# The opening of a two-layer transformer trunk: who sums the modulation weights, and in which number format the first projection runs

## The chip, the cores and the metric

The program runs on one core of a Trainium2 chip. The metric is the device time of one execution in microseconds (us). The kernel before was timed in three runs: median 2475.24 us, lowest 2470.18, highest 2477.14.

## What is computed

Two layers work on 256 tokens of 2048 features in float32. Every sub-layer normalises its input, multiplies it by a scale and adds a shift, and the scales and shifts come from a conditioning vector `c` through a large matrix `ada_w`. The opening of the program is the first of these steps and the projection behind it:

```
mod = einsum('bd,lde->lbe', silu(c), ada_w) + ada_b        # (2 layers) x 2048 x 12288
shift_m, scale_m, gate_m, shift_f, scale_f, gate_f = split(mod[layer], 6)
h = rmsnorm(x, norm_g[layer, 0]) * (1 + scale_m) + shift_m
proj = h @ a_w_in                                          # 2048 -> 512 + 256 + 128 + 16
q_lat, c_kv, k_idx, w_idx = split(proj)                    # each but the last is normalised
q_idx = q_lat @ a_w_idx_qb                                 # the indexer's queries, 16 heads
...                                                        # selection of keys, attention, MLP, layer 1
```

For layer 0 the opening needs the columns of `ada_w` that give `shift_m` and `scale_m`: 2048 rows by 4096 columns, 32 transfers of 1024 KB. `a_w_in` adds 16 pieces of 456 KB and `x` 8 pieces of 256 KB.

## The kernel before, in words

Everything is unrolled in one function, `trunk`. A library orders the instructions of each engine, gives each tile its memory and places the waits. Each engine then runs its own list in order, and the transfers are issued from the list of SyncE (SP).

**The opening** goes through the features in eight segments of two chunks (`SEG = 2`, a chunk is 128 features). One `step` loads 8 chunks of rows (`ROWS`) of 256 columns of `ada_w` for one part (scale or shift) of a segment: one transfer of 1024 KB (`start_load`, L501), five steps ahead of its use (`LEAD`), into one of six buffers. There are 32 steps, four per segment. `start_sum` then weighs the rows with silu(c) and adds them up. VectorE (DVE) takes four of the eight rows of a step (`ROWS_DVE`), one instruction per row of 128x256 (`add_row`, L206 for the first, L208 after it). TensorE (PE) takes the other four as matmuls that give one row of 256 sums (`row`, L511).

When a segment's sums are done, `start_columns` copies the row out of PSUM (ScalarE, L525) and `ada_columns` brings both kinds of sums into columns by tiny matmuls (`col`, L227 and L228), after which VectorE adds the bias and forms gain times (1 + scale) (`mod`, L229 and L232). `start_project` modulates the transposed x (`xT`) of the two chunks. `start_product` multiplies them with `a_w_in`.

The product comes in two forms. For the first twelve chunks (`LATE = 12`) the weights and the features are each split into a high and a low part in the format float32r (`halves` and `split`: L131 on ScalarE, L132 on VectorE), and three matmuls stand for one (L553 to L555). For the last four chunks the matmul is in plain float32 (L546). The results collect in PSUM: `pq` (512 columns) and `pk` (400 columns) for two token tiles each.

**Behind the opening** the tiles of the opening's pool are given back (`sp_.close()`), and layer 0's attention begins. For each of the two token tiles the loop from L625 on takes the norm of `pq`, transposes it and splits it into `qlat`. In the same pass it does the same for the keys' part in `pk` (`ckv`, `kidx`). The power in `inv_rms` runs on GpSimd (POOL, L139), which also issues the transfers of the position bias (L736). Then the indexer loops over four units of `a_w_idx_qb`: `unit` fetches two raw tiles (`fetch`, L106; four raw buffers in all), splits them (L131, L132), and lets the `Filler` tick. The filler spreads the sums for all later modulations over the program: its loads `adaw` are 512 KB each (L272), its sums are VectorE instructions of 128x1024 (L208). The products of the unit with `qlat` are `qi` (L126 to L128), and `dots` (L678) needs `kidx`.

Of the kernel before, what the change touches and what calls it, by code (L numbers as in the profile page):

```python
# [39 lines left out]
SEG = 2  # L40
ROWS = 8
ROWS_DVE = 4
LATE = 12
# [3 lines left out]
def trunk(ctx: ExitStack, tc: tile.TileContext, x, c, rel_bias, ada_w, ada_b, norm_g, a_w_in, a_q_norm,  # L47
# [14 lines left out]
    # ---------------------------------------------------------------- constants  # L62
# [30 lines left out]
    # ---------------------------------------------------------------- weights  # L93
# [48 lines left out]
    # ---------------------------------------------------------------- per-feature columns  # L142
# [16 lines left out]
    banks(f=(0, 1), m=(2, 3), lg=(4, 5), s=(6,), av=(7,), row=(4, 5, 7))  # L159
# [32 lines left out]
    # relative position bias by distance, then by (query, key)  # L192
# [7 lines left out]
    # ---------------------------------------------------------------- adaLN  # L200
# [9 lines left out]
    def ada_columns(l, p, c0, acc, row=None):  # L210
        """Columns c0 .. of part p (shift, or gain * (1 + scale)) from sums by partition and a row to add."""
# [5 lines left out]
        if row is None:  # L217
            for j in range(0, n, 4):
                ps = small_ps("col")
                for k in range(4):  # L220
                    nc.tensor.transpose(ps[:, k * P:(k + 1) * P], acc[:, (j + k) * P:(j + k + 1) * P], ident)
                nc.vector.reduce_sum(col[:, j:j + 4], ps.rearrange("p (a b) -> p a b", a=4), axis=AX.X)
            sums = col
        else:
            sums = small_ps("col")[:, :n]
            for k in range(n):
                nc.tensor.matmul(sums[:, k:k + 1], acc[:, k * P:(k + 1) * P], ones[:, 0:1], start=True, stop=False)  # L227
                nc.tensor.matmul(sums[:, k:k + 1], row[0:1, k * P:(k + 1) * P], ones[0:1, 0:1], start=False, stop=True)  # L228
        nc.vector.tensor_add(col, sums, bcols[l][:, p * NC + k0:p * NC + k0 + n])  # L229
# [4 lines left out]
    def ada_gate(l, p, c0, acc):  # L234
        """Columns c0 .. of a gate times the norm's gain, in every partition."""
# [20 lines left out]
    class Filler:  # L256
        """Spreads the sums over ada_w's rows between the units of weights; its loads run ahead."""
# [64 lines left out]
    def m_piece(u, xk, ps_tiles, n, tiles=range(NT)):  # L322
        """ps_tiles[t] (tokens, features) += x @ W over u: a list of (k, high, low)."""
# [71 lines left out]
    def x_transposed(r, j, half, tag, xn):  # L395
        """Features (4 * j + 2 * half) * 128 .. of the normalised x, transposed: [P, 2, tokens] in PSUM."""
# [18 lines left out]
    def next_h(a, b):  # L415
        """Tiles for the modulated, normalised x, transposed; and what fills them when a token tile of x is done."""
# [37 lines left out]
    def quiet(what="hold"):  # L454
        """What comes in here waits until the next features are on their way."""
# [17 lines left out]
    def first_products(ps_tiles, ws):  # L473
        """ps_tiles[t] = x @ W over the first chunks, in plain float32, which needs no parts."""
# [7 lines left out]
    # ---------------------------------------------------------------- start: layer 0's first modulation and projection  # L482
    hts = [sp.tile([P, 4, 2, T], F32R, tag=f"h{j}", name=uid("h")) for j in range(LATE // 4)]
# [4 lines left out]
    acc, prow, wa = {}, {}, {}  # L488
    raws = {}
# [3 lines left out]
    SW = SEG * P  # L493
    steps = [(g, p, k) for g in range(NC // SEG) for k in range(0, NC, ROWS) for p in (1, 0)]
    last_step = {g: i for i, (g, _, _) in enumerate(steps)}

    def start_load(i):
        g, p, k = steps[i]
        c0 = p * D + g * SW
        wa[i] = sp.tile([P, ROWS, SW], F32, tag="w", name=uid("w"), bufs=LEAD + 1)  # L500
        nc.sync.dma_start(out=wa[i], in_=rows(ada_w[0], k, k + ROWS, c0, c0 + SW))  # L501

    def start_sum(i):
        g, p, k = steps[i]
        if k == 0:
            acc[g, p] = sp.tile([P, BLK], F32, tag="acc", name=uid("acc"), bufs=4)
            prow[g, p] = small_ps("row", "row")
        for j in range(ROWS_DVE):
            add_row(acc[g, p][:, :SW], wa[i][:, j], k + j, cs)
        for j in range(ROWS_DVE, ROWS):  # L510
            nc.tensor.matmul(prow[g, p][0:1, :SW], cs[:, k + j:k + j + 1], wa[i][:, j],  # L511
                             start=(k == 0 and j == ROWS_DVE), stop=(k + j == NC - 1))

# [8 lines left out]
    def start_columns(g):  # L522
        for p in (1, 0):
            row = sp.tile([1, BLK], F32, tag="row", name=uid("row"), bufs=2)
            nc.scalar.activation(row[:, :SW], prow[g, p][0:1, :SW], AF.Copy)  # L525
            ada_columns(0, p, g * SW, acc[g, p][:, :SW], row)

    def start_project(g):
        a, b = mods[0, 1], mods[0, 0]
        for k in range(g * SEG, (g + 1) * SEG):  # L530
            if k >= LATE:
                modulate(k, h_late[:, k - LATE], xT[:, k], a[:, k:k + 1], b[:, k:k + 1])
                waiting.append((k,))
                continue
            hi, lo = win.pop(k)
            hv = hts[k // 4][:, k % 4]
            h32 = work.tile([P, T], F32, tag="h32", name=uid("h32"))
            modulate(0, h32, xT[:, k], a[:, k:k + 1], b[:, k:k + 1])
# [531 lines left out]
```

## Time and profile before

| What | Value |
|---|---|
| median of three runs | 2475.24 us (2470.18 to 2477.14) |
| span of the profiled execution | 2471.3 us |
| PE / PE weight loads | 98% / 84% of the span |
| DVE / ACT / POOL | 69% / 49% / 2% |
| transfers | 614.21 MB, 249 GB/s over the span |

The span runs from the first to the last instruction of one profiled execution. The page gives no time of its own for that execution beside the span; the median of the timed runs is 3.9 us above it. Busy shares are averages over the span, and PE's ends are modelled. In the rows below, PEld is the loading of weights into TensorE, SPq is a transfer's issue on SyncE, and PEclk is the granted clock of TensorE as a share of its full speed.

### The profile page before, as it was taken

How to read it: one execution, taken by the hardware profiler on the slowest of the kernel's cores; microseconds unless marked ns; L12 is line 12 of the kernel's file. 1: busy time of each engine (PE TensorE's matmuls, PEld its weight loads, DVE VectorE, ACT ScalarE, POOL GpSimd, SP SyncE). 2: the span in 40 equal slices, each digit the busy share in tenths (PEclk: the TensorE clock that was granted, in tenths of full speed). 3: DMA queues.
4: the chain of work that ended last, by engine and by line, in shares of the span. 5: the costliest groups of instructions: out<-in, count | busy, mean ns of one | idle time of the engine just before them, and what ended most of it. 6: DMA issues, size and time to landing. Idle time of an engine off the chain costs nothing.

```text
span 2471.3 us, 37142 instructions
## 1 busy us (share of the span) xinstructions
PE 2409.8 (98%) x14540; PEld 2077.5 (84%) x14540; DVE 1699.2 (69%) x2147; ACT 1203.0 (49%) x1717; POOL 48.5 (2%) x86
## 2 busy tenths in 40 slices
PE   7989999999999999999999999999999999999998
PEld 4559788877988989989977989887898998988986
DVE  5669888888566766766568668877854456655455
ACT  4135755556444444444446554446654444444443
POOL 0010000000000000000000000000000000000000
PEclk9999999999999999999999999999999999999999
DMA  9967988875778878878566788886676557766564
GB/s 354 311 229 244 328 272 308 299 248 196 260 232 280 286 252 294 282 260 283 186 206 208 256 279 322 325 314 221 220 247 191 183 189 240 241 189 187 183 189 145
DMA packets 294472, 614.21 MB, mean 249 GB/s; under 512 B 19492, under 2 KB 60792, under 8 KB 294296
## 3 DMA queue, kind: packets, MB, share of 16 engines
q1 hardware_dynamic: 290464, 603.14, 72.5%
q0 software_dynamic: 3168, 8.53, 1.2%
q8 instruction: 114, 1.87, 0.3%
q14 instruction: 62, 0.51, 0.1%
q10 hardware_dynamic: 664, 0.17, 0.0%
HBM read 609.62 MB, written 2.15 MB: 248 GB/s over the span
## 4 chain that ended last, share of the span: by engine, by line
PE 60%; DVE 3%; DMA 3%; ACT 2%; issue 1%; POOL 0%; SPq 0%; DVEq 0%; POOLq 0%; ACTq 0%
PE m L331 9%; PE m L330 9%; PE m L329 9%; PE f L128 7%; PE f L126 7%; PE f L127 7%; PE pq L128 1%; PE pq L126 1%; PE pq L127 1%; DMA adaw<-in_ada_w_dram 1%; PE pk L128 1%; PE pk L127 1%; PE pk L126 1%; DVE wlo L132 1%; DMA raw<-in_b_w_out_dram 1%
## 5 line engine op out<-in xcount | busy, mean ns | idle before, releaser
L132 DVE TENSOR_TENSOR wlo<-raw,whi 128x1024 fp32r<-128x1024 f32 (+1 forms) x738 | 886.3, 1219 | 447.3 <-ACT whi L131 442.4
L131 ACT ACTIVATE whi<-raw 128x1024 fp32r<-128x1024 f32 (+1 forms) x738 | 767.4, 1055 | 852.4 <-PE f L127 328.3
L128 PE MATMUL f<-h,wlo 128*128 128x256 f32 x1920 | 541.6, 282 | 0.0
L126 PE MATMUL f<-h,whi 128*128 128x256 f32 x1920 | 541.4, 282 | 0.0
L127 PE MATMUL f<-h,whi 128*128 128x256 f32 x1920 | 540.8, 282 | 0.0
L208 DVE SCALAR_TENSOR_TENSOR acc<-adaw,cs,acc 128x1024 f32<-128x1024 f32 x300 | 384.2, 1281 | 74.4 <-DMA adaw<-in_ada_w_dram 71.6
L331 PE MATMUL m<-wlo,hid 128*128 128x512 f32 x1016 | 401.2, 395 | 0.5 <-DVE wlo L132 0.5
L329 PE MATMUL m<-whi,hid 128*128 128x512 f32 x1016 | 401.2, 395 | 0.0
L330 PE MATMUL m<-whi,hid 128*128 128x512 f32 x1016 | 400.8, 395 | 0.0
L127 PEld LDWEIGHTS f<-h,whi 128*128 128x128 f32 x1920 | 361.8, 188 | 1.5
L126 PEld LDWEIGHTS f<-h,whi 128*128 128x128 f32 x1920 | 361.9, 188 | 1.2
L128 PEld LDWEIGHTS f<-h,wlo 128*128 128x128 f32 x1920 | 361.5, 188 | 0.0
L331 PEld LDWEIGHTS m<-wlo,hid 128*128 128x128 f32 x1016 | 191.2, 188 | 46.7 <-DVE wlo L132 1.7
L330 PEld LDWEIGHTS m<-whi,hid 128*128 128x128 f32 x1016 | 191.2, 188 | 43.9
L329 PEld LDWEIGHTS m<-whi,hid 128*128 128x128 f32 x1016 | 191.2, 188 | 43.6
L363 DVE TENSOR_TENSOR y<-m,y 128x512 f32<-128x512 f32 x200 | 136.6, 685 | 31.9 <-PE m L331 31.7
L329 PE MATMUL m<-whi,o 128*128 128x512 f32 x368 | 150.2, 408 | 0.0
L331 PE MATMUL m<-wlo,o 128*128 128x512 f32 x368 | 146.9, 401 | 0.2 <-DVE wlo L132 0.2
L330 PE MATMUL m<-whi,o 128*128 128x512 f32 x368 | 147.0, 399 | 0.0
L331 PEld LDWEIGHTS m<-wlo,o 128*128 128x128 f32 x368 | 69.3, 189 | 15.1 <-DVE wlo L132 0.6
L329 PEld LDWEIGHTS m<-whi,o 128*128 128x128 f32 x368 | 69.6, 189 | 13.5 <-ACT qkv L723 0.3
L330 PEld LDWEIGHTS m<-whi,o 128*128 128x128 f32 x368 | 69.5, 189 | 13.3
(289 smaller groups left out, 3043.6 us busy)
## 6 DMA issues: line engine op xcount, KB each, us to landing
raw<-in_mlp_w_dram SPq DMA_DIRECT2D x504, 512.0 KB, 4.7
adaw<-in_ada_w_dram SPq DMA_DIRECT2D x320, 512.0 KB, 6.4
raw<-in_b_w_in_dram SPq DMA_DIRECT2D x92, 512.0 KB, 5.4
w<-in_ada_w_dram SPq DMA_DIRECT2D x32, 1024.0 KB, 7.1
raw<-in_a_w_out_dram SPq DMA_DIRECT2D x64, 512.0 KB, 5.8
raw<-in_b_w_out_dram SPq DMA_DIRECT2D x32, 512.0 KB, 7.2
raw<-in_a_w_qb_dram SPq DMA_DIRECT2D x16, 512.0 KB, 5.4
raw<-in_a_w_in_dram SPq DMA_DIRECT2D x12, 456.0 KB, 7.3
```

The costliest lines, as they stand in the source:

```text
L126: nc.tensor.matmul(o, sh, mh, start=start, stop=False, skip_group_check=True)
L127: nc.tensor.matmul(o, sh, ml, start=False, stop=False, skip_group_check=True)
L128: nc.tensor.matmul(o, sl, mh, start=False, stop=stop, skip_group_check=True)
L131: return (nc.scalar.activation(dst_hi, src, AF.Copy).ins, nc.vector.tensor_sub(dst_lo, src, dst_hi.bitcast(F32)).ins)
L132: nc.vector.tensor_sub(dst_lo, src, dst_hi.bitcast(F32)).ins)
L208: nc.vector.scalar_tensor_tensor(acc, w, cs[:, k:k + 1], acc, op0=ALU.mult, op1=ALU.add)
L329: nc.tensor.matmul(o, xh[:, ts_], hi, start=(k == 0), stop=False)
L330: nc.tensor.matmul(o, xl[:, ts_], hi, start=False, stop=False)
L331: nc.tensor.matmul(o, xh[:, ts_], lo, start=False, stop=(k == n - 1))
L363: nc.vector.tensor_add(y, pt[d][t], y)
```

## The change

The opening is rewritten. VectorE sums all rows, except the last chunk of rows, which goes to TensorE. A segment now holds four chunks of features (three segments) or two (the last two), and scale and shift stand side by side, so that one instruction adds 1024 columns, or 512 in the last two segments. A step still fills one buffer of 1024 KB, now by two transfers of 512 KB; the last two steps are half as large. `a_w_in` comes in one transfer per segment into two buffers, and all its products are in plain float32, one chunk after each step (two in the short segments). The first two units of `a_w_idx_qb` are fetched and split at the end of the opening, and the norms of `pq` go ahead of those of `pk`. The remaining lines of the diff only take out comments.

```diff
-SEG = 2
-ROWS = 8
-ROWS_DVE = 4
-LATE = 12
+SEGS = ((0, 4), (4, 4), (8, 4), (12, 2), (14, 2))
...
+    for g, (_, n) in enumerate(SEGS):
+        r = 8 // n
+        rs = [r] * (NC // r) if g < len(SEGS) - 1 else [r] * (NC // r - 1) + [r // 2] * 2
+        steps += [(g, sum(rs[:i]), r_) for i, r_ in enumerate(rs)]
...
     def start_load(i):
+        g, k, r = steps[i]
+        k0, n = SEGS[g]
+        w = sp.tile([P, 4 * BLK], F32, tag="w", name=uid("w"), bufs=LEAD + 1)
+        wa[i] = w[:, :2 * r * n * P].rearrange("p (r a n) -> p r a n", r=r, a=2)
+        for p in range(2):
+            c0 = p * D + k0 * P
+            nc.sync.dma_start(out=wa[i][:, :, p], in_=rows(ada_w[0], k, k + r, c0, c0 + n * P))
+
+    def start_w_in(g):
+        k0, n = SEGS[g]
+        w = sp.tile([P, 4, WIN], F32, tag="win", name=uid("win"), bufs=2)
+        nc.sync.dma_start(out=w[:, :n], in_=rows(a_w_in[0], k0, k0 + n, 0, WIN))
...
     def start_sum(i):
+        on_pe = 1 if i == len(steps) - 1 else 0
...
+        for j in range(r - on_pe):
+            add_row(a_, wa[i][:, j].rearrange("p a n -> p (a n)"), k + j, cs)
+        for j in range(r - on_pe, r):
+            for c_ in range(2 * n):
+                nc.tensor.matmul(ps[:, c_:c_ + 1], wa[i][:, j, c_ // n, (c_ % n) * P:(c_ % n + 1) * P],
+                                 cs[:, k + j:k + j + 1], ...)
+        if last:
+            for c_ in range(2 * n):
+                nc.tensor.matmul(ps[:, c_:c_ + 1], a_[:, c_ * P:(c_ + 1) * P], ones[:, 0:1], ...)
...
+    def start_h(g):
+        nc.vector.tensor_add(mod[:, :, ks], acc[g][1][:, :2 * n].rearrange(...), b_)
+        nc.vector.scalar_tensor_tensor(mod[:, 1, ks], mod[:, 1, ks], 1.0, gcol[:, ks], op0=ALU.add, op1=ALU.mult)
+        h = sp.tile([P, 4, T], F32, tag="h", name=uid("h"), bufs=2)
+        for i in range(n):
+            modulate(i if n == 2 else 1, h[:, i], xT[:, k], mod[:, 1, k:k + 1], mod[:, 0, k:k + 1])
+
+    def start_product(k, o, w_, c0, t):
+        nc.tensor.matmul(o[t][:, :w_], h32s[k][:, t * P:(t + 1) * P], win[k][:, c0:c0 + w_],
+                         start=(k == 0), stop=(k == NC - 1))
...
     for i in range(len(steps) + LEAD):
         if i < len(steps):
             start_load(i)
+            g, k, _ = steps[i]
+            if k == 4:
+                start_w_in(g)
...
         start_sum(done)
+        g = steps[done][0]
+        if done - 1 == last_step.get(g - 1):
+            start_h(g - 1)
+            waiting += range(SEGS[g - 1][0], sum(SEGS[g - 1]))
+        for _ in range(1 if SEGS[g][1] == 4 else 2):
+            if waiting:
+                k = waiting.pop(0)
+                for t in range(NT):
+                    for o in outs:
+                        start_product(k, *o, t)
...
+    start_h(len(SEGS) - 1)
+    waiting += range(SEGS[-1][0], NC)
+    for o in outs:
+        for t in range(NT):
+            for k in waiting:
+                start_product(k, *o, t)
+    qi_units = [halves(fetch(rows(a_w_idx_qb[0], 0, 4, u * BLK, (u + 1) * BLK), 4, BLK), 4, BLK) for u in range(2)]
     sp_.close()
```

## Rows read from the trace of the kernel before

**Rows 1.** The page, part 1: busy time, share of the span and instructions of each engine.
```profile
PE 2409.8 (98%) x14540; PEld 2077.5 (84%) x14540; DVE 1699.2 (69%) x2147; ACT 1203.0 (49%) x1717; POOL 48.5 (2%) x86
```
**Rows 2.** Stretches: length, busy us of PE, PEld, DVE, ACT, POOL, PEclk, DMA share, GB/s.
```profile
2.00:40.00 38.00, 27.00 (x107) 13.89 (x108) 18.75 (x52) 19.98 (x42) 3.43 (x9) 0.87 1.06 376
40.00:120.00 80.00, 75.36 (x356) 43.98 (x354) 51.15 (x118) 15.67 (x30) 0.55 (x1) 1.00 0.95 326
140.00:150.00 10.00, 9.13 (x37) 3.98 (x35) 2.30 (x7) 1.88 (x4) 0.00 (x0) 1.00 0.00 0
154.00:156.00 2.00, 2.00 (x4) 1.01 (x3) 1.47 (x2) 0.02 (x1) 0.00 (x0) 0.52 0.73 205
```
**Rows 3.** Transfers in 160 to 170 us, slices of 0.25 us and issues.
```profile
DMA packets 1144, 3.81 MB, mean 381 GB/s; under 512 B 145, under 2 KB 145, under 8 KB 1144
...
adaw<-in_ada_w_dram SPq DMA_DIRECT2D x2, 512.0 KB, 5.4
```
**Rows 4.** SyncE's waits in 0 to 260 us: total, times, longest.
```profile
SPq L501 <- DVE acc L208: 44.8, 18, 4.5
...
SPq L501 <- PE row L511: 28.5, 12, 4.0
```
**Rows 5.** DVE's waits in 40 to 120 us: total, times, longest.
```profile
DVE mod L229 <- PE col L228: 26.4, 10, 4.8
```
**Rows 6.** Groups by shape in 0 to 160 us: busy, mean ns, idle before.
```profile
L511 PE MATMUL row<-w,cs 128*1 128x256 f32 x256 | 64.2, 396 | 1.4 <-DMA w<-in_ada_w_dram 1.4
L208 DVE SCALAR_TENSOR_TENSOR acc<-w,cs,acc 128x256 f32<-128x256 f32 x112 | 53.1, 483 | 2.8
...
L132 DVE TENSOR_TENSOR wlo<-raw,whi 128x1024 fp32r<-128x1024 f32 x4 | 4.8, 1221 | 0.0
```
**Rows 7.** Groups by shape, DVE, 30 to 180 us: the filler's sums.
```profile
L208 DVE SCALAR_TENSOR_TENSOR acc<-adaw,cs,acc 128x1024 f32<-128x1024 f32 x6 | 7.7, 1278 | 0.0
```
**Rows 8.** Timeline of SyncE: start, us, the issues of the opening's end.
```profile
90.99 13.45 SPq L501 DMA_DIRECT2D w<-in_ada_w_dram  x4
...
123.30 0.38 SPq L501 DMA_DIRECT2D w<-in_ada_w_dram  x1
123.78 32.09 SPq L106 DMA_DIRECT2D raw<-in_a_w_idx_qb_dram  x8
```
**Rows 9.** Timeline of 118 to 185 us: the end of the opening.
```profile
123.20 0.50 PE L553 MATMUL pq<-whi,h 128*128 128x512 f32 x1
...
125.88 1.89 PE L511 MATMUL row<-w,cs 128*1 128x256 f32 x8
127.69 0.30 PEld L227 LDWEIGHTS col<-ones,acc 128*128 128x128 f32 x2 [0.44 <-issue]
...
140.85 1.12 PE L546 MATMUL pq<-win,h_late 128*128 128x512 f32 x2
...
144.11 1.89 PE L511 MATMUL row<-w,cs 128*1 128x256 f32 x8
...
151.53 0.60 ACT L410 ACTIVATE h_late<-xT,mod,mod 128x256 f32<-128x256 f32 x1 [0.78 <-DVE mod L229]
...
152.00 1.61 PE L546 MATMUL pq<-win,h_late 128*128 128x512 f32 x2 [0.70 <-DVE h_late L411]
...
157.91 0.60 ACT L625 ACTIVATE sq<-pq 128x512 f32<-128x512 f32 x1 [3.89 <-PE pq L546]
```
**Rows 10.** Timeline of 160 to 200 us: the norms and the first products behind them.
```profile
160.09 1.50 POOL L736 DMA_DIRECT2D bias<-tab_d  x2
...
163.06 0.69 DVE L132 TENSOR_TENSOR qlat<-h,qlat 128x512 fp32r<-128x512 f32 x1
...
168.47 0.68 DVE L132 TENSOR_TENSOR qlat<-h,qlat 128x512 fp32r<-128x512 f32 x1
...
169.21 0.58 PE L127 MATMUL qi<-qlat,whi 128*128 128x256 f32 x1 [0.91 <-DVE qlat L132]
...
176.56 1.47 PE L678 MATMUL dots<-misc,qkv 128*128 128x128 f32 x8
```

More of the change, by code (lines that the diff above doesn't have):

```diff
@@ L216, in ada_columns @@
         col = mods[l, p][:, k0:k0 + n]
[L217 to L229, printed above, removed]
+        for j in range(0, n, 4):
+            ps = small_ps("col")
+            for k in range(4):
+                nc.tensor.transpose(ps[:, k * P:(k + 1) * P], acc[:, (j + k) * P:(j + k + 1) * P], ident)
+            nc.vector.reduce_sum(col[:, j:j + 4], ps.rearrange("p (a b) -> p a b", a=4), axis=AX.X)
+        nc.vector.tensor_add(col, col, bcols[l][:, p * NC + k0:p * NC + k0 + n])
         if p in (1, 4):
@@ L487, in trunk @@
     pk = [bank("f", "pk") for _ in range(NT)]
[L488 to L495, printed above, removed]
-    def start_load(i):
[L498 to L501, printed above, removed]
+    mod = const.tile([P, 2, NC], F32, name="mod_start")
@@ L503, in start_sum @@
+    def start_w_in(g):
+        k0, n = SEGS[g]
+        w = sp.tile([P, 4, WIN], F32, tag="win", name=uid("win"), bufs=2)
+        nc.sync.dma_start(out=w[:, :n], in_=rows(a_w_in[0], k0, k0 + n, 0, WIN))
+        win.update((k0 + i, w[:, i]) for i in range(n))
     def start_sum(i):
-        g, p, k = steps[i]
+        g, k, r = steps[i]
+        n = SEGS[g][1]
+        on_pe = 1 if i == len(steps) - 1 else 0
         if k == 0:
-            acc[g, p] = sp.tile([P, BLK], F32, tag="acc", name=uid("acc"), bufs=4)
-            prow[g, p] = small_ps("row", "row")
@@ L508, in start_sum @@
[L508 to L512, printed above, removed]
+            acc[g] = (sp.tile([P, 2 * BLK], F32, tag="acc", name=uid("acc"), bufs=2)[:, :2 * n * P],
+                      bank("col", "col"))
+        a_, ps = acc[g]
+        for j in range(r - on_pe):
+            add_row(a_, wa[i][:, j].rearrange("p a n -> p (a n)"), k + j, cs)
@@ new lines, in start_sum @@
+        last = i == last_step[g]
+        for j in range(r - on_pe, r):
+            for c_ in range(2 * n):
+                nc.tensor.matmul(ps[:, c_:c_ + 1], wa[i][:, j, c_ // n, (c_ % n) * P:(c_ % n + 1) * P],
+                                 cs[:, k + j:k + j + 1], start=(c_ == 0), stop=False,
+                                 skip_group_check=True)
+        if last:
+            for c_ in range(2 * n):
+                nc.tensor.matmul(ps[:, c_:c_ + 1], a_[:, c_ * P:(c_ + 1) * P], ones[:, 0:1],
+                                 start=(on_pe == 0 and c_ == 0), stop=True, skip_group_check=True)
@@ L520, in start_x @@
                 nc.scalar.activation(xT[:, 4 * j + 2 * half:4 * j + 2 * half + 2], ps, AF.Copy)
[L522 to L538, printed above, removed]
-            split(hv[:, 0], hv[:, 1], h32)
-            waiting.append((k, hi, lo))
@@ L599, in trunk @@
             nc.gpsimd.dma_start(out=tab_d, in_=tab)
-        if done == 1:
-            *bcols, gcol, qncol = [columns(*r_) for r_ in small_rows]
-    while waiting:
-        start_product(*waiting.pop(0))
+    start_h(len(SEGS) - 1)
[5 more added lines that the diff above has]
+    qi_units = [halves(fetch(rows(a_w_idx_qb[0], 0, 4, u * BLK, (u + 1) * BLK), 4, BLK), 4, BLK) for u in range(2)]
     sp_.close()
@@ L620, in trunk @@
     widx = const.tile([P, NT, HI], F32, name="widx")
+    sums = [small.tile([P, NB], F32, tag="ss", name=uid("ss")) for _ in range(NT)]
     for t in range(NT):
         tsl = slice(t * P, (t + 1) * P)
-        ss = small.tile([P, NB], F32, tag="ss", name=uid("ss"))
+        ss = sums[t]
         sq = work.tile([P, BLK], F32, tag="sq", name=uid("sq"), bufs=1)
         nc.scalar.activation(sq, pq[t], AF.Square, accum_out=ss[:, 0:1])
-        nc.scalar.activation(sq[:, :KVR], pk[t][:, :KVR], AF.Square, accum_out=ss[:, 1:2])
         r = inv_rms(ss[:, 0:1], QR)
@@ L635, in trunk @@
         split(qlat[:, :, 0, tsl], qlat[:, :, 1, tsl], h32)
+    for t in range(NT):
+        tsl = slice(t * P, (t + 1) * P)
+        ss = sums[t]
+        sq = work.tile([P, BLK], F32, tag="sq", name=uid("sq"), bufs=1)
+        nc.scalar.activation(sq[:, :KVR], pk[t][:, :KVR], AF.Square, accum_out=ss[:, 1:2])
         r = inv_rms(ss[:, 1:2], KVR)
@@ L667, in trunk @@
     for u in range(4):
-        parts = unit(rows(a_w_idx_qb[0], 0, 4, u * BLK, (u + 1) * BLK), 4, BLK, 1.5)
+        if u < len(qi_units):
+            parts = qi_units[u]
+            filler.tick(1.5)
+        else:
+            parts = unit(rows(a_w_idx_qb[0], 0, 4, u * BLK, (u + 1) * BLK), 4, BLK, 1.5)
         pf = [bank("f", "qi") for _ in range(2)]
```

63 lines of the change are left out of this document (19 added, 44 removed).

## The prediction

> **What bounds the kernel now.** I read the busy shares first: TensorE is busy for 98% of the span [rows 1], so a stretch saved ahead of it is kept unless another engine takes over. Then the stretches of the opening. From 2 to 40 us the transfers run at 376 GB/s, from 40 to 120 us at only 326, and from 140 to 150 us at nothing, though the opening's products are not done [rows 2]. So the opening is not bound by its bytes alone. The waits of SyncE say what holds them: its issues of ada_w's pieces wait 44.8 us for VectorE's sums and 28.5 us for TensorE's row matmuls, the two readers that must let go of a buffer [rows 4]. TensorE is the late one of them: 75 of 80 us busy from 40 to 120 [rows 2], VectorE 51, and VectorE itself stands 26.4 us waiting for column matmuls [rows 5] that lie behind TensorE's other work. A segment takes (123.30 - 90.99) / 2 = 16.2 us [rows 8].
>
> At the end this becomes a tail. The last piece of ada_w is issued at 123.30 [rows 8], but TensorE still works off row matmuls and products (125.88, 140.85, 144.11), the last features are modulated at 151.53, and ScalarE reads the first finished `pq` at 157.91 [rows 9]. The indexer's products run without a break from 169.21 on [rows 10]. The raw buffers are full meanwhile, hence the 10 us without transfers.
>
> **What the change does to the engines.** TensorE loses the row matmuls, 64.2 us [rows 6], and the columns of their rows. A chunk's products cost 125.88 - 123.20 = 2.68 us in three float32r matmuls and 144.11 - 140.85 = 3.26 in plain float32 [rows 9], so twelve chunks cost 12 x 0.58 = 7 us more. All sixteen make 52 us, far under the opening's length.
>
> VectorE loses 53.1 us of sums [rows 6] with the splitting of w_in, and gains 48 sums of 1024 columns at 1.28 us [rows 7] and 32 of 512. The latter has no row; between 0.48 us for 256 [rows 6] and 1.28 for 1024, a straight line gives 0.75. Together 61 + 24 = 85 us, which fits under the transfers if these take 115. In a long segment it is 20.5 us of sums against 27 of transfers, in a short one 12 against 13.6.
>
> **The stream.** 33.6 MB of ada_w, 7.5 of a_w_in and 2.1 of x are 43.1 MB. With TensorE no longer holding buffers I take the 376 GB/s of 2 to 40 us, when buffers were free [rows 2]. That is 115 us, an end at 117. The lower bound is 326 GB/s: an end at 134. SyncE issues 66 transfers for ada_w instead of 32, and 5 for a_w_in instead of 16; at 0.38 us for an issue [rows 8] that is some 27 us of its 117, covered. The pieces become 512 KB: the filler's pieces of that size, beside others, ran at 381 GB/s [rows 3]. (The Trainium skill, "DMA: Bandwidth & Descriptors", section "Bandwidth", says to batch transfers to 1 MiB or more and gives 341 GB/s for that size; by that figure the end would be at an estimated 128 us. Rows 3 speak against it.)
>
> **The last segments, step by step.** At 376 GB/s the long segments land at 35 (x is in the first), 62 and 89.5 us, the short ones at 103 and 117. Third segment: two sums, 2.6 us, to 92.1. Eight column matmuls at 0.30 [rows 9], 2.4, to 94.5. The modulation about 1 us: 0.47 from its start to the product [rows 9] and 0.5 allowed for the two small VectorE steps ahead of it. So its four chunks start at 95.5 and take 13 us, plus 2 because TensorE begins at half clock after a slack stretch (0.52 in 154 to 156 us [rows 2]; the products from 152.00 ran slow for 4 us [rows 9]). TensorE is through at 110.5.
>
> Here the change adds a wait. a_w_in has two buffers, and the fifth segment's piece needs the third segment's. On SyncE's queue stand behind it the last three pieces of ada_w, 2.1 MB. With the 0.9 MB of a_w_in they take 8 us plus some 2 to the landing, from 110.5 to 121 instead of 117. The fourth segment's columns also wait for those products; its two chunks then run from about 112.5 to 119.
>
> From 121: one sum on VectorE 0.75, four columns 1.2, modulation 1, two matmuls of `pq` 1.7 (about half a chunk): the first `pq` is done at 125.7, against 157.91 before. That is **32 us**.
>
> **What follows it.** The first two indexer units are split (4.8 us on VectorE [rows 6]) beside the last 6.5 us of products; before, this also lay ahead of the norms. If the cover went, up to 4.8 us would come onto the path. SyncE's queue has them behind ada_w's last piece, as before, and the filler's loads now come ahead of units 2 and 3, which are needed some 20 us later. From `pq` to unbroken products it is 169.21 - 157.91 = 11.3 us now. One token tile's own chain takes 163.75 - 157.91 = 5.8 [rows 9, 10]; with the second some 2 us behind, 8 would do, so the new order can bring 0 to 3.5. I take 0: `dots`, 7.4 us behind the first product [rows 10], needs the keys' norms, which now come last, so TensorE may stop there instead. POOL's bias issues, 1.5 us for two [rows 10], can come between its powers as they do now: 0 to 1.5 either way.
>
> Sum: 2475.24 - 32.2 = **2443 us** for the median, or 2439 for a span like the 2471.3 of the profiled execution, which is 3.9 us under the median.
>
> **The rivals.**
> *Half clock throughout.* Bursts of products with idle stretches between never bring TensorE to full speed; a chunk costs 6.5 us. The third segment's products then end at 121.5, the last pieces land at 131.6, the next two chunks end at 136.6, columns and modulation at 138.7, and `pq` is done at 142.2. Gain 15.7: 2459.5. For it: the 0.52 [rows 2]. Against it: full clock returned after 4 us of products [rows 9], and a burst lasts 13. (The Trainium skill, "TensorE: Matmul & The Clock Gate", section "HAM oscillation — how this bites in real kernels", describes every burst behind a wait for transfers as starting slow, which speaks against this change; the trace agrees for the start of one.) Chance 0.10.
>
> *The stream is no faster.* The buffers were not what held it, or the smaller transfers cost: 326 GB/s, end at 134, and 4.7 to 6.4 us to `pq` (the upper figure at half clock). Gain 17 to 19: 2457. For it: VectorE's waits are the larger part of rows 4. Against it: 376 and 381 [rows 2, 3]. Chance 0.13.
>
> *Sums and products run one after the other (the other side).* VectorE runs in order: if at each segment's end it stands at `mod` for columns that lie behind products on TensorE, as the 26.4 us show it can [rows 5], nothing overlaps. A long segment is then 20.5 + 2.4 + 1 + 13 = 37 us, a short one 12 + 1.2 + 1 + 6.5 = 20.7, in all 7 for the first landing + 111 + 41 - 4.8 (only `pq` of the last) = 154: no change that can be measured. It decides against the change from a chunk of 3.5 us on; at half clock it is 47 us more, `pq` at 201, slower by 43: 2518. Against it: the next segment's first sums are written ahead of that wait, and TensorE is idle at two of the three long ends. Chance 0.04 for no change, 0.06 for slower.
>
> *The gain is given back* in the indexer, where the filler's sums crowd VectorE: no change, chance 0.04. Against it: VectorE has the same work there, and it begins earlier by as much.
>
> **How the numbers follow.** Forecast 0.63, half clock 0.10, no faster stream 0.13, in series 0.10, given back 0.04. The forecast's own range: without the hold for a_w_in's buffer 4 us better, with the norms' 3.5 another, and 3 for the spread of the runs, down to 2432; up to 2450 with the splits uncovered and POOL's 1.5. The range reaches to the first two rivals: **2432 to 2460**, with about 0.86 inside by the cases. Faster by over 0.3% (7.4 us, about what a measurement of this kernel can tell): 0.63 + 0.10 + 0.13 = 0.86. Within: 0.08. Slower: 0.06.
>
> **What the changed profile would show.** Right: over 360 GB/s from 20 to 100 us; SyncE's longest wait of the opening at a_w_in's last piece, for TensorE; the last sum on VectorE at about 122 us, `pq` read at about 126, unbroken `qi` products from about 137; behind that, the same profile 32 us earlier. A chunk's four matmuls at 3.3 us, sums of 512 columns near 0.75. Wrong: transfers under 340 GB/s with SyncE waiting for VectorE (stream), a granted clock near 0.5 over whole bursts (half clock), `mod` waiting over 10 us for `col` (series), or VectorE without gaps behind the opening and TensorE waiting for it (given back).

## The result, and the profile after

The changed kernel's median is **2443.19 us** (four runs, 2442.82 to 2450.8), beside 2472.87 for the kernel before (the three runs named at the start and a fourth, 2470.5): a ratio of 0.9885, with a 95% interval of 0.9871 to 0.9899. The profiled execution's span is 2441.4 us, 29.9 less than the span before. With the fourth run the median of the kernel before lies 2.4 us under the 2475.24 from which the forecast was counted.

The busy shares of the changed kernel's page, first (busy us, share of the span, instructions):

```profile
PE 2354.8 (96%) x14180; PEld 2048.3 (84%) x14180; DVE 1703.6 (70%) x2048; ACT 1189.1 (49%) x1689; POOL 46.9 (2%) x86
```

TensorE has lost 55 us of work against [rows 1] and VectorE gained 4, the direction the change was meant to have. Next the opening in stretches (columns as in [rows 2]: length, busy us of PE, PEld, DVE, ACT, POOL, granted clock, DMA share, GB/s):

```profile
20.00:40.00 20.00, 9.99 (x34) 5.90 (x34) 14.64 (x12) 8.43 (x14) 0.00 (x0) 1.00 1.05 408
...
60.00:80.00 20.00, 14.27 (x39) 8.76 (x40) 15.35 (x15) 2.08 (x4) 0.00 (x0) 0.74 1.05 410
80.00:100.00 20.00, 12.69 (x33) 7.53 (x32) 15.71 (x19) 2.07 (x4) 0.00 (x0) 0.67 1.07 395
100.00:110.00 10.00, 10.00 (x30) 5.16 (x28) 6.11 (x9) 0.00 (x0) 0.00 (x0) 0.98 0.42 147
126.00:128.00 2.00, 1.91 (x3) 0.88 (x4) 1.77 (x3) 1.18 (x2) 0.00 (x0) 0.50 0.56 127
```

The stream runs at about 400 GB/s from 20 to 100 us, where it made 326 from 40 to 120 us before [rows 2], and then nearly stops: 147 GB/s from 100 to 110. TensorE stands idle for a third to a half of the time in the three stretches of 20 us shown. By the profile the granted clock is 1.00 in the first of them all the same, 0.74 and 0.67 on average in the others, and 0.50, the lower of its two levels, from 126 to 128. Who holds the stream is told by the waits (engine line waited for: total us, times, longest; SyncE's over 0 to 230 us, VectorE's over 0 to 135):

```profile
SPq L497 <- DVE acc L205: 12.1, 12, 2.3
...
SPq L502 <- PE pk L548: 11.1, 1, 11.1
...
DVE mod_start L539 <- PE col L523: 16.6, 5, 4.4
```

Against [rows 4], SyncE's wait for VectorE's sums went from 44.8 us to 12.1, that for row matmuls is gone, and one long wait is new: 11.1 us for the products of the third segment. SyncE's own list shows it (start, us, issues):

```profile
87.10 11.66 SPq L497 DMA_DIRECT2D w<-in_ada_w_dram  x8
109.94 0.37 SPq L502 DMA_DIRECT2D win<-in_a_w_in_dram  x1
110.40 3.54 SPq L497 DMA_DIRECT2D w<-in_ada_w_dram  x6
113.99 19.20 SPq L103 DMA_DIRECT2D raw<-in_a_w_idx_qb_dram  x8
```

Nothing is issued from 98.8 to 109.94, and the last six issues of `ada_w` stand behind. The timeline of all engines, from the third segment's end to the first read of `pq` and on to the indexer (start, us, idle time before and its releaser in brackets):

```profile
93.38 0.17 DVE L539 TENSOR_TENSOR mod_start<-col,b_col 128x8 f32<-128x8 f32 x1 [3.73 <-PE col L523]
...
93.66 0.48 DVE L203 TENSOR_SCALAR acc<-w,cs 128x512 f32<-128x512 f32 x1
...
94.51 2.07 PE L548 MATMUL pq<-win,h 128*128 128x512 f32 x2 [1.17 <-ACT h L400]
...
103.63 1.02 PE L548 MATMUL pq<-win,h 128*128 128x512 f32 x2
...
109.75 0.95 PE L523 MATMUL col<-ones,acc 128*128 128x1 f32 x8
...
112.72 1.12 PE L548 MATMUL pq<-win,h 128*128 128x512 f32 x2 [2.02 <-DVE h L401]
...
117.59 5.48 DVE L205 SCALAR_TENSOR_TENSOR acc<-w,cs,acc 128x512 f32<-128x512 f32 x7 [1.11 <-DMA w<-in_ada_w_dram]
...
124.48 1.23 DVE L129 TENSOR_TENSOR wlo<-raw,whi 128x1024 fp32r<-128x1024 f32 x1
...
125.63 0.41 DVE L401 TENSOR_SCALAR h<-xT,mod_start 128x256 f32<-128x256 f32 x1
...
126.09 6.17 PE L548 MATMUL pq<-win,h 128*128 128x512 f32 x8 [1.92 <-DVE h L401]
...
129.91 0.60 ACT L615 ACTIVATE sq<-pq 128x512 f32<-128x512 f32 x1 [2.73 <-PE pq L548]
...
134.78 0.60 PE L621 MATMUL qT<-ident,xn 128*128 128x128 f32 x4
...
141.51 0.56 PE L124 MATMUL qi<-qlat,whi 128*128 128x256 f32 x1
...
148.72 0.38 PE L675 MATMUL dots<-misc,qkv 128*128 128x128 f32 x2
```

The same `pq` product of one tile (two records) takes 2.07 us at the burst's start and 1.02 in its middle. Against [rows 9, 10], `pq` is read 28.0 us earlier (157.91 to 129.91) and `dots` starts 27.8 earlier (176.56 to 148.72). So the gain is made in the opening, and the indexer's start keeps it. Not all of it is earlier work: the last product of the opening ends 25.1 us earlier (160.08 to 134.94 in the two traces), and `pq` gains more because the last two chunks are now multiplied for both tiles of `pq` first and for `pk` after that.

### The profile page after: what moved, and what is told of

The parts are those of the page before. It is cut to its first block, busy times and chain, and to the rows that moved or that the text cites. A ratio compares the mean times of both kernels' runs of the same rounds, so it can differ in the third digit from the quotient of the medians.

```text
span 2441.4 us, 36310 instructions
## 1 busy us (share of the span) xinstructions
PE 2354.8 (96%) x14180; PEld 2048.3 (84%) x14180; DVE 1703.6 (70%) x2048; ACT 1189.1 (49%) x1689; POOL 46.9 (2%) x86
## 4 chain that ended last, share of the span: by engine, by line
PE 64%; ACT 2%; DVE 2%; DMA 1%; issue 1%; POOL 0%; DVEq 0%; POOLq 0%; SPq 0%; ACTq 0%
PE m L321 9%; PE m L320 9%; PE m L319 9%; PE f L123 8%; PE f L125 8%; PE f L124 8%; PE pq L123 1%; PE pq L125 1%; PE pq L124 1%; PE pv L319 1%; PE pv L320 1%; PE pv L321 1%; PE pk L123 1%; PE pk L125 1%; PE pk L124 1%; DMA adaw<-in_ada_w_dram 1%
## 5 line engine op out<-in xcount | busy, mean ns | idle before, releaser
L129 DVE TENSOR_TENSOR wlo<-raw,whi 128x1024 fp32r<-128x1024 f32 x726 | 873.9, 1221 | 448.6 <-ACT whi L128 442.2
L128 ACT ACTIVATE whi<-raw 128x1024 fp32r<-128x1024 f32 x726 | 756.7, 1057 | 860.6 <-PE m L320 329.5
L205 DVE SCALAR_TENSOR_TENSOR acc<-w,cs,acc 128x1024 f32<-128x1024 f32 (+1 forms) x74 | 79.6, 1075 | 10.9 <-DMA w<-in_ada_w_dram 8.6
L319 PEld LDWEIGHTS m<-whi,o 128*128 128x128 f32 x368 | 69.8, 190 | 13.6 <-ACT qkv L720 0.6
```

Of the source, the lines that this page charges most:

```text
L128: return (nc.scalar.activation(dst_hi, src, AF.Copy).ins, nc.vector.tensor_sub(dst_lo, src, dst_hi.bitcast(F32)).ins)
L129: nc.vector.tensor_sub(dst_lo, src, dst_hi.bitcast(F32)).ins)
L205: nc.vector.scalar_tensor_tensor(acc, w, cs[:, k:k + 1], acc, op0=ALU.mult, op1=ALU.add)
L319: nc.tensor.matmul(o, xh[:, ts_], hi, start=(k == 0), stop=False)
```

## The experiments

Two questions are put: which part of the change makes the 28 us, and what sets the opening's end now. Where an expectation gives a price for the whole kernel, the scatter of its runs (2442.82 to 2450.8 for the changed kernel) mostly hides it, so `pq`'s first read is compared too. The medians of the kernel before beside them were 2472.32, 2473.78 and 2473.78 us in the three sessions. The changed kernel ran again in the second (e8, one run) and the third (e11).

### Which part makes the gain

**e3: the kernel before, with all rows on VectorE, still 256 columns at a time.**

```diff
-ROWS_DVE = 4
+ROWS_DVE = 8
```

(and the row's matmul, copy and second column matmul taken out.)

> The kernel before, with VectorE summing all eight rows of each step and no row matmuls; segments, 256 columns an instruction, split products as before. Theory (the width of 1024 columns is what lets VectorE carry all sums): 256 sums at 0.51 us are 131 us, and with the splitting and modulating of before, about 24 us, VectorE needs 155 us and more; the last sum comes at 160 to 165 us and the kernel is 8 to 15 us slower than the kernel before: 2481 to 2488. Rival (relieving TensorE is enough): the transfers run at over 370 GB/s and it is 15 to 25 us faster than before: 2448 to 2458.

Measured: 2471.42 us, ratio 0.9997 (0.9986 to 1.0008): no change. Its stretch of 40 to 120 us, columns as above:

```profile
40.00:120.00 80.00, 41.63 (x148) 34.18 (x146) 76.70 (x192) 10.40 (x17) 0.55 (x1) 0.71 0.91 311
```

VectorE is busy 76.7 of 80 us and the stream is at 311 GB/s: the bound moved from TensorE to VectorE, as expected. The expected loss of 8 to 15 us did not come, though: `pq` is read at 160.98, 3.1 us later than before, and the total doesn't show it. Relieving TensorE alone, at 256 columns, is worth nothing.

**e4: the kernel before, with all products in plain float32.**

```diff
-LATE = 12
+LATE = 0
```

(and six buffers for the unsplit pieces of `a_w_in`.)

> The kernel before, with all sixteen chunks of a_w_in's product in plain float32 and no splits of its weights; the sums are shared between VectorE and TensorE as before. Theory (TensorE bounds the opening of before): twelve chunks cost 0.58 us more each on the bound engine, so it is 3 to 7 us slower than the kernel before: 2476 to 2480. Rival (the splits on VectorE and ScalarE hold the opening, and plain float32 is itself a gain): 5 to 15 us faster: 2458 to 2468.

Measured: 2488.76 us, ratio 1.0068 (1.0048 to 1.0088), 16 us slower, more than expected. The same stretch, one of its waits and one of its groups (busy, mean ns, idle before):

```profile
40.00:120.00 80.00, 74.67 (x271) 32.10 (x269) 31.82 (x80) 5.38 (x12) 0.55 (x1) 0.94 0.82 279
```
```profile
DVE mod L229 <- PE col L228: 84.9, 16, 10.9
```
```profile
L511 PE MATMUL row<-w,cs 128*1 128x256 f32 x256 | 71.6, 431 | 1.5 <-DMA w<-in_ada_w_dram 1.5
```

VectorE is relieved (31.8 us against 51 in [rows 2]) but stands 84.9 us, in sixteen waits over the whole opening, for columns behind TensorE's longer products (in the kernel before such waits come to 48.9 us in sixteen; the 26.4 of [rows 5] are those from 40 to 120 us), and the stream falls to 279 GB/s. The total lost more than twice the 7 us that the dearer products were priced at. The row matmuls also took 431 ns each, not 396 as in [rows 6], which is 7.4 us more on TensorE; the granted clock was 0.94 from 40 to 120 us, where the kernel before had 1.00.

**e5: the changed kernel, with three float32r products and their splits.**

```diff
-        nc.tensor.matmul(o[t][:, :w_], h32s[k][:, t * P:(t + 1) * P], win[k][:, c0:c0 + w_], ...)
+        hi, lo, hv = halved[k]
+        xh, xl = hv[:, 0, t * P:(t + 1) * P], hv[:, 1, t * P:(t + 1) * P]
+        nc.tensor.matmul(o[t][:, :w_], xh, hi[:, c0:c0 + w_], start=(k == 0), stop=False)
+        nc.tensor.matmul(o[t][:, :w_], xl, hi[:, c0:c0 + w_], start=False, stop=False)
+        nc.tensor.matmul(o[t][:, :w_], xh, lo[:, c0:c0 + w_], start=False, stop=(k == NC - 1))
```

> The changed kernel with the products of before: every chunk of a_w_in and of the features split into two float32r parts, three matmuls for one. Theory (plain float32 buys VectorE the room for all the sums): a chunk takes 2.7 us instead of 3.3 on TensorE, but VectorE gets 16 splits of 1.10 us and 16 of 0.42, some 24 us on top of its 85, at the chunks' ends where the sums are due; the last sum comes 5 to 15 us later and the kernel is 5 to 15 us slower than the changed one: 2448 to 2458. Rival (plain float32 only costs TensorE time, and TensorE sets the end): the third segment's products end 2 us earlier and it is 1 to 3 us faster: 2440 to 2442.

Measured: 2476.49 us, ratio 1.001 (0.9994 to 1.0025). The whole gain is gone, about twice the upper end of what I expected: `pq` is read at 157.78, where the kernel before had 157.91. Its waits, and two groups of VectorE's:

```profile
SPq L497 <- DVE acc L205: 68.1, 23, 8.6
...
ACT whi L128 <- PE pk L562: 24.5, 11, 3.8
```
```profile
L129 DVE TENSOR_TENSOR wlo<-win,whi 128x912 fp32r<-128x912 f32 x16 | 17.6, 1106 | 15.3 <-ACT whi L128 15.3
...
L129 DVE TENSOR_TENSOR hv<-h,hv 128x256 fp32r<-128x256 f32 x16 | 6.1, 419 | 0.5 <-ACT hv L128 0.5
```

I had counted the splits' 24 us of VectorE. I had not counted the chain behind them: VectorE idles 15.3 us for the high parts from ScalarE, ScalarE waits 24.5 us for the part tiles to come free of TensorE's products, and VectorE's sums stand behind in order. SyncE then waits 68.1 us for the sums. In this run's source a chunk is split just ahead of its product, into one of four part tiles; the kernel before splits the weights some steps earlier. Whether an earlier place or more part tiles would keep some of the gain was not tried.

So the 28 us need both halves, as they are built here: the rows off TensorE (e4 without that is slower) and the splits off VectorE (e3 and e5 without that gain nothing). All rows on VectorE at 256 columns together with plain products was not tried, nor were the longer segments and the 512 KB transfers by themselves, so what the width and these bring stays open.

### What sets the opening's end now

**e1: the changed kernel, with a buffer of its own for the last piece of `a_w_in`.**

```diff
+        if g == len(SEGS) - 1:
+            w = sp.tile([P, n, WIN], F32, name="win_last")
+        else:
             w = sp.tile([P, 4, WIN], F32, tag="win", name=uid("win"), bufs=2)
```

> The changed kernel, with a buffer of its own for the last segment's piece of a_w_in. Theory (the opening's end is set by TensorE's products of the third segment, not by the bytes): SyncE's 11.1 us wait for TensorE goes and the last piece of ada_w lands about 10 us earlier, but the fourth segment's columns still stand behind the third's products and VectorE's mod still waits for them, some 4 us; the last sum comes at about 121 us instead of 123.1, and the kernel gains 1 to 3 us: 2440 to 2442. Rival (the held transfers set the end): the last sum comes 8 to 10 us earlier and so does everything behind it: 2433 to 2435.

Measured: 2444.62 us, ratio 0.9885 (0.9869 to 0.9902), as the changed kernel: neither the 1 to 3 us of the theory nor the 8 to 10 of the rival. The long wait of SyncE is gone and the piece is issued at 100.15. But (timeline):

```profile
109.96 0.95 PE L526 MATMUL col<-ones,acc 128*128 128x1 f32 x8
...
112.79 9.41 DVE L205 SCALAR_TENSOR_TENSOR acc<-w,cs,acc 128x512 f32<-128x512 f32 x12
...
129.05 0.60 ACT L618 ACTIVATE sq<-pq 128x512 f32<-128x512 f32 x1 [2.73 <-PE pq L551]
```

The fourth segment's columns still come at 109.96, behind the third's products, and VectorE then has twelve sums to catch up on. These run without a break to 122.20 (the changed kernel: 123.07). The bytes are there earlier, and nobody can use them. The wait that I had priced at 4 us is worth 0.9 at `pq`, less than the 2 us by which three executions of the changed kernel itself differ there (129.91, 130.21 in e8, 131.90 in e11).

**e2: matmuls that nobody reads, ahead of the third segment's columns and the last ones, to hold the clock up.**

```diff
+        if (g == 2 and i >= last_step[g] - 3) or i >= len(steps) - 2:
+            warm_ps = bank("av", "warm")
+            for _ in range(2):
+                nc.tensor.matmul(warm_ps, ident, wt[i][:, :BLK], start=True, stop=True)
```

> The changed kernel, with twelve matmuls more whose results nobody reads, in the stretches where TensorE had nothing to do ahead of the third segment's columns and ahead of the last ones. Theory (half clock is part of the chain): the third segment's products take 13.2 us instead of 15.2, the transfer behind them is issued 2 us earlier, the last pq products begin nearer to full clock and end up to 1.7 us earlier; together 2 to 4 us faster: 2439 to 2441. Rival (the clock doesn't matter here, or the added matmuls delay the columns by their own 1.7 us): 2443 to 2445.

Measured: 2449.41 us, ratio 0.9912 (0.9897 to 0.9927), no gain. The timeline:

```profile
91.53 1.84 PE L528 MATMUL col<-ones,acc 128*128 128x1 f32 x16
...
94.54 2.08 PE L553 MATMUL pq<-win,h 128*128 128x512 f32 x2 [1.17 <-ACT h L400]
...
109.89 0.95 PE L528 MATMUL col<-ones,acc 128*128 128x1 f32 x8
```

The columns ran at full speed (1.84 us, not 3.54), but the burst 1.2 us behind them began as slowly as ever (2.08 for the first `pq`) and took 15.3 us. The granted clock was 1.00 from 90 to 92 us and 0.50 from 94 to 100. At the end the added matmuls stood in front of the last columns (125.11, where the changed kernel has 123.12), as the rival had it; the last burst took 5.4 us instead of 6.2, and `pq` was read at 131.65. The added matmuls did not buy the long burst's start; what a start at full clock would be worth remains unmeasured.

**e7: the third segment cut into two of two chunks.**

```diff
-SEGS = ((0, 4), (4, 4), (8, 4), (12, 2), (14, 2))
+SEGS = ((0, 4), (4, 4), (8, 2), (10, 2), (12, 2), (14, 2))
```

> The changed kernel with its third segment of four chunks cut into two of two, so that no burst of products is longer than 6.5 to 8 us. Theory (the third segment's burst of four chunks sets the end, through a_w_in's buffer on SyncE and the column matmuls behind it): SyncE no longer waits there for more than 3 us, the stream runs at 400 GB/s to about 110 us, pq is read at 114 to 119 us instead of 129.9, and the kernel is 10 to 15 us faster than the changed one: 2428 to 2434. Rival (VectorE's sums, now 90 us, or the bytes set the end anyway): less than 4 us: 2439 to 2443.

Measured: 2449.14 us, ratio 0.9887 (0.9861 to 0.9913); `pq` at 131.25. A miss. Its SyncE wait, and one stretch:

```profile
SPq L502 <- PE pk L548: 17.1, 3, 10.9
```
```profile
75.00:90.00 15.00, 12.97 (x39) 6.86 (x38) 10.70 (x18) 0.60 (x1) 0.00 (x0) 0.95 0.57 194
```

More segments mean more pieces of `a_w_in` in the same two buffers, so the hold merely comes earlier, at 75 to 90 us, and the sums of 512 columns, two for one of 1024, end at 125.4.

**e9: the changed kernel with e1's buffer, and `mod` issued after the first step of the next segment's sums.**

```diff
-        nc.vector.tensor_add(mod[:, :, ks], acc[g][1][:, :2 * n].rearrange(...), b_)
+        with tc.issue_after(added[0]):
+            nc.vector.tensor_add(mod[:, :, ks], acc[g][1][:, :2 * n].rearrange(...), b_)
```

> The changed kernel with a buffer of its own for the last segment's piece of a_w_in, and with VectorE's mod of a segment queued behind the next segment's first step of sums, two rows of 1024 or four of 512. Theory (VectorE's order sets the end: it stands 3.7 us at mod at the end of each long segment and 4.4 at the fourth's while the columns are made, since mod lies ahead of the next sums in its list): about 2.5 us less wait at each of the three long ends and 2 to 3 at the fourth's, TensorE's third burst begins some 4 us earlier, and pq is read at 122 to 126 us instead of 129.9. The kernel is 4 to 8 us faster than the changed one. Rival (the waits are covered, since VectorE then waits for transfers instead): pq at 128 to 130 and no difference.

Measured: 2443.33 us, ratio 0.9875 (0.9859 to 0.9892). The changed kernel in the same session (e11) made 2448.6, ratio 0.9895 (0.9878 to 0.9911). The intervals overlap, so these runs don't show it to be faster. Two waits of VectorE's:

```profile
DVE acc L204 <- DMA w<-in_ada_w_dram: 12.3, 7, 4.4
DVE mod_start L542 <- PE col L525: 10.2, 5, 3.1
```

The wait for columns in e1, which has the same buffer (all three over 0 to 135 us):

```profile
DVE mod_start L542 <- PE col L526: 15.4, 5, 3.7
```

The timeline of e9:

```profile
111.79 7.05 DVE L204 SCALAR_TENSOR_TENSOR acc<-w,cs,acc 128x512 f32<-128x512 f32 x9
...
111.93 2.07 PE L551 MATMUL pq<-win,h 128*128 128x512 f32 x2 [2.07 <-DVE h L400]
...
119.72 0.95 PE L520 MATMUL col<-cs,w 128*128 128x1 f32 x8
...
127.31 0.60 ACT L618 ACTIVATE sq<-pq 128x512 f32<-128x512 f32 x1 [2.73 <-PE pq L551]
```

VectorE's wait falls from 16.6 us to 10.2, its sums end at 118.84 instead of 123.07, and `pq` comes at 127.31, 2.6 us under the earliest of the three executions of the changed kernel. Part of that is e1's buffer: beside e1 the late `mod` takes the wait from 15.4 to 10.2 and brings `pq` 1.7 us forward (129.05 to 127.31), less than the 2 us of scatter. And while it waits 5.2 us less for columns, VectorE stands 4.4 us longer for transfers (12.3 against 7.9 in e1), as the rival said. `pq` also comes later than the expected 122 to 126, partly because now TensorE is the late one, its fourth segment's products from 111.93 to 119.72 being in front of the last columns.

**e10: e9's order, e7's segments, five buffers of two chunks for `a_w_in`, one chunk after each step.**

```diff
-        w = sp.tile([P, 4, WIN], F32, tag="win", name=uid("win"), bufs=2)
+        for j in range(0, n, 2):
+            w = sp.tile([P, 2, WIN], F32, tag="win", name=uid("win"), bufs=5)
...
-        for _ in range(1 if SEGS[g][1] == 4 else 2):
+        for _ in range(1):
```

> The same late mod, with the third segment cut into two short ones, a_w_in in five buffers of two chunks, so that SyncE waits for no products, and one chunk of products after each step. Theory (VectorE's order and TensorE's bursts together set the end): the stream runs without a stop to about 112 us, the last sum ends at 113 to 117 us, and pq is read at 119 to 123 instead of 129.9; 7 to 11 us faster than the changed kernel. Rival (the sums of 512 columns cost VectorE what the waits did): pq at 126 to 130, under 4 us.

Measured: 2446.28 us, ratio 0.9883 (0.9869 to 0.9898), `pq` at 127.84: a miss, in the rival's range of 126 to 130. SyncE no longer waits for products at all, and the end is where e9 has it: the chunks of features 12 and 13 run from 111.20 to 120.4.

### The order behind the opening, and the rest of the program

**e6: the changed kernel without the early splits, and with the norms in the old order.**

```diff
-    qi_units = [halves(fetch(rows(a_w_idx_qb[0], 0, 4, u * BLK, (u + 1) * BLK), 4, BLK), 4, BLK) for u in range(2)]
+    qi_units = []
...
         nc.scalar.activation(sq, pq[t], AF.Square, accum_out=ss[:, 0:1])
+        nc.scalar.activation(sq[:, :KVR], pk[t][:, :KVR], AF.Square, accum_out=ss[:, 1:2])
```

(and the second pass over `pk` taken out.)

> The changed kernel without its two changes behind the sums: the first two indexer units are fetched in their loop again, and each token tile's pq and pk norms go together again. Theory (these carry nothing of the gain, since the splits ran ahead of the norms before too): from the first reading of pq to the unbroken qi products 11 to 13 us instead of 11.6, total 2442 to 2447. Rival (part of the gain is theirs): 3 to 8 us longer there, total 2446 to 2452.

**e8: the changed kernel again, beside e6.**

> The changed kernel once more, for its profile. Theory (what differs behind the opening, 4 us in layer 1's attention, belongs to the program, as its engines meet its transfers there in the same way each time): the stretch from the first norm at the end of layer 0 to the first norm at the end of layer 1's attention takes 426 us again, within 1 us. Rival (it differs from execution to execution): it differs by 2 us or more.

Measured: 2449.65 us for e6, ratio 0.9893 (0.986 to 0.9926), and 2449.82 for e8. The two timelines, e6 first:

```profile
130.06 0.60 ACT L615 ACTIVATE sq<-pq 128x512 f32<-128x512 f32 x1 [2.73 <-PE pq L548]
...
144.21 0.58 PE L124 MATMUL qi<-qlat,whi 128*128 128x256 f32 x1 [0.18 <-DVE qlat L129]
...
152.23 1.47 PE L671 MATMUL dots<-misc,qkv 128*128 128x128 f32 x8
```
```profile
130.21 0.60 ACT L615 ACTIVATE sq<-pq 128x512 f32<-128x512 f32 x1 [2.73 <-PE pq L548]
...
142.66 0.56 PE L124 MATMUL qi<-qlat,whi 128*128 128x256 f32 x1
...
149.98 0.38 PE L675 MATMUL dots<-misc,qkv 128*128 128x128 f32 x2
```

From nearly the same read of `pq`, the new order reaches unbroken products 1.5 us and `dots` 2.3 us sooner. From `pq` to unbroken products e6 takes 14.2 us, over the theory's 11 to 13; the changed kernel takes 11.6, 12.5 and 11.6 in its three executions. In the total two such microseconds don't show.

**e11: the changed kernel a third time, timed beside e9 and e10.**

> The changed kernel beside these two on the same chip, for the comparison. Theory and rival: pq is read at 129.9 to 130.2 us again; the total lies anywhere from 2443 to 2450, since the stretches behind the opening have differed by 1 to 3 us each between its executions.

Measured: 2448.6 us, ratio 0.9895 (0.9878 to 0.9911), `pq` at 131.90, where 129.9 to 130.2 was expected. e8 and e11 allow the program to be compared with itself. The table gives the lengths of four stretches, each the difference between the starts of the first power `r` on POOL in two sub-layers:

| | `pq`'s norm to layer 0's MLP | to layer 1 | to its MLP | to the last norm |
|---|---|---|---|---|
| before | 391.8 | 739.8 | 430.2 | 737.9 |
| after | 394.3 | 739.5 | 426.0 | 738.1 |
| after, e8 | 397.0 | 742.6 | 427.3 | 737.3 |
| after, e11 | 394.3 | 739.2 | 429.0 | 736.9 |

One and the same program differs by up to 3.4 us in a stretch. So the 4.2 us that the third stretch won in the profiled execution can't be given to the change; e8 was expected to repeat its 426.0 within 1 us and has 427.3, and e11 with 429.0 has the difference that the rival foretold. The first stretch was longer in all three, by 2.5 to 5.2. A single 391.8 is a weak base: e3 and e4, whose source behind the opening is that of the kernel before, have 388.6 and 393.8 there. But these two and the 391.8 average 391.4 and those of the changed kernel 395.2, so some 4 us seem to be given back in this stretch. VectorE now has three of the filler's sums (1.27 us each) inside layer 0's selection of keys, whose two masks on POOL lie 27.3 us apart instead of 24.5; but TensorE, which has other products to do there, waits 2.5 us for the mask (with its weight load) instead of 2.1. Whether that is the whole of it was not tried.

## Why the prediction was right, and where its steps were off

The total was forecast at 2443 and came at 2443.19. That it came so close is luck: **the opening gave 28.0 us, not 32.2**; 1.9 us came from behind it in the profiled pair, where the table shows that the executions differ by more than that; and the base of the forecast fell by 2.4 us with a fourth run. The last two make up for the 4.2 that the opening lacks. All nine runs of the changed kernel lie between 2442.82 and 2450.8, with a median of 2448.17, and in the two later sessions it gained 24.0 us (one run) and 25.2. That fits 28 us in the opening less some 4 given back in the stretch behind it, so the rival *the gain is given back* seems true for a small part. The direction, the range and most of the mechanism held.

| Step | forecast | measured |
|---|---|---|
| stream, GB/s | 376 | 408 to 410 (20 to 80 us), 395 |
| third segment's products | 95.5 to 110.5 | 94.51 to 109.75 |
| last piece of `a_w_in` issued | 110.5 | 109.94 |
| fourth segment's products | 112.5 to 119 | 112.72 to 120.64 |
| last sum ends | 121.75 | 123.07 |
| `pq` done or read | 125.7 | 129.91 |
| `pq` to unbroken `qi` | 11.3 | 11.6 |

**What held.** The diagnosis: the two readers, not the bytes, held the stream. The prices: a sum of 512 columns 751 ns (0.75 by the straight line), one of 1024 columns 1284; a chunk in plain float32 3.06 us (two tiles, 103.63 to 106.69) at full clock, where I had 3.26. The added wait for `a_w_in`, found in its place to 0.6 us. But the third segment's products began within 1 us of the forecast by two misses that cancel: the last sum ended at 89.65, not 92.1, since the stream was faster, and the columns took 3.5 us, not 2.4. VectorE's groups, busy, mean ns and idle before:

```profile
L205 DVE SCALAR_TENSOR_TENSOR acc<-w,cs,acc 128x1024 f32<-128x1024 f32 x45 | 57.8, 1284 | 8.9 <-DMA w<-in_ada_w_dram 7.5
...
L205 DVE SCALAR_TENSOR_TENSOR acc<-w,cs,acc 128x512 f32<-128x512 f32 x29 | 21.8, 751 | 2.0 <-DMA w<-in_ada_w_dram 1.1
```

The rival of a stream that is no faster falls with the 408 GB/s. (The Trainium skill, "DMA: Bandwidth & Descriptors", section "Bandwidth", gives 341 GB/s for transfers of 1 MB, issued there from GpSimd; this stream, most of it in transfers of 512 KB, stayed above that figure for 60 us.)

**What was mis-sized: the last step**, "From 121: one sum on VectorE 0.75, four columns 1.2, modulation 1, two matmuls of `pq` 1.7". The last sum ended 1.3 us late, because VectorE, which had a landing at 117.59, then ran seven sums without a break to 123.07: the rest lay there faster than it could be summed. The last piece itself had landed at about 120.1 (issued at 113.5, with 6.6 us to the landing), where I had 121. The columns took 1.1. The modulation, from 124.21 to the product at 126.09, took 1.9, since a split of the indexer's weights (124.48, 1.23 us) stands ahead of `h` in VectorE's list: the splits that I had costed at nothing, beside the products, are partly in front of them. And the products took 3.8 us to the read at 129.91. Two matmuls of `pq` at full clock are 2.04 (twice 1.02), so "about half a chunk" was 0.3 short; the other 1.8 are the lower clock (0.50 from 126 to 130). I had allowed that for the third segment's burst and not for this one. Together 1.3 - 0.1 + 0.9 + 2.1 = 4.2, the whole error at `pq`.

**What was mis-placed.** Against the rival in series the prediction said "the next segment's first sums are written ahead of that wait". In the source they are (`start_sum` of the next step stands before `start_h`). But the library orders VectorE's list, and there `mod` stands ahead of all the next sums at the three long ends: VectorE waits 3.7 us in `mod` (93.38) before it starts the sums of the fourth segment (93.66), and 16.6 us in five such waits. That is over the 10 us which the prediction itself had named as the sign of this rival. So the sign was set too low: the rival's mechanism is there, but sums and products still overlap, since TensorE is idle at the long ends, as the same sentence said (their columns wait for VectorE's last sum, not the other way round). Beside e1, e9 bought back 5.2 us of these waits and 1.7 at `pq`.

**The hold for `a_w_in`'s buffer** was priced at 4 us in the forecast's own range. e1 took it away and `pq` came 0.9 earlier, within the scatter. The term was right as a wait and wrong as a price: behind it stands the same burst of TensorE, which also delays the fourth segment's columns.

**Half clock throughout** didn't come true, but its first part did: in each of the three executions, the three long bursts began with a `pq` at twice its time and came down to 1.02 for it 3 to 6 us later, and the last burst's eight `pq` records took 6.2 to 6.7 us, where eight in a row at 1.02 for two would be some 4. (The Trainium skill, "TensorE: Matmul & The Clock Gate", section "HAM oscillation — how this bites in real kernels", says this of bursts that wait for transfers; the trace agrees for the starts of these bursts, which wait for VectorE's sums.) One thing stays open: in the first long burst the profile grants the full clock (1.00 from 44 to 47 us), though the sixteen records of columns ahead of it took 3.57 us and its first `pq` 2.08.

**The norms and early splits**, taken at 0 within 0 to 3.5, were worth 1.5 to 2.3 us (e6 against e8). They don't show beside the kernel before (11.6 us from `pq` to unbroken products, 11.3 before) because of TensorE's own list. Before, the products ended 2.2 us behind the first read of `pq`, and the first transposes (`qT`) began 2.3 us behind it, at 160.22. Now the products of the second tile and of `pk` still stand ahead of the transposes, whose input is ready at 132.16: they begin at 134.78, 4.9 us behind the read.

## What to carry to other kernels

When two engines both read what a stream brings, relieving one of them can move the wait to the other: e3 took the rows off TensorE and gained nothing, e4 took the splits off VectorE and lost 16 us. The change does both, with wider instructions, and brought 28 us in the opening. Where a segment's last step is a chain over engines that run in order, list everything that stands in each engine's list between the last landing and the end, and price the first matmuls of a burst there at what such starts measured (2.07 us for a product of one tile instead of 1.02). A long wait in a queue is worth only what the next late thing leaves: taking away the 11.1 us wait moved `pq` by 0.9. And a forecast that comes within 0.2 us of one median is no proof of its terms.

## What was not expected of the hardware

From 20 to 80 us a stream of forty transfers of 512 KB and two of 1824 KB ran at 408 to 410 GB/s on this one core, above every stretch of [rows 2, 3]. Matmuls ahead of a burst did not carry the full clock over: in e2 eight us of added matmuls, sixteen records of columns at full speed and a pause of 1.2 us were followed by a burst that started slow again. And the same program, executed again, varies by up to 2 us at the end of its opening and by up to 3.4 us in one later stretch, so a difference of 2 us in one trace is no finding.
